# The last residual of a fused diffusion layer: new row factors, and tiles dealt out anew to three engines

## The chip, the cores and the metric

The program runs on one core of a Trainium2 chip. The metric is the device time of one launch, in microseconds (us), as a median over runs. The engines are named as in the profile: PE is TensorE (PEld its weight loads), DVE is VectorE, ACT is ScalarE, POOL is GpSimd, and SP is the engine that here only issues DMA transfers.

## What is computed

One layer of a hybrid backbone over 384 tokens (128 context, 256 latent) of width 2048: modulation, a mixing sub-layer, and a SwiGLU feed-forward sub-layer. Only its last line matters here:

```python
ff = (jax.nn.silu(h @ lw['w_ffn_gate']) * (h @ lw['w_ffn_up'])) @ lw['w_ffn_down']
x = x + ga2 * rmsnorm(ff, lw['norm_post_ffn'])
```

with `rmsnorm(x, g) = x * rsqrt(mean(x * x) + EPS) * g`, the mean over the 2048 channels of a token. So each token needs one factor, 1/sqrt(mean of ff squared), and every channel of that token is multiplied by it before it is added to x.

## The kernel before

Everything is held transposed: channels on the 128 partitions, the 384 tokens along the free dimension. A tensor of 2048 channels is 16 tiles of 128x384 fp32, written `x1(k)` (the residual) and `acc(k)` (the accumulated FFN output), k = 0 to 15. Both live in SBUF in two halves of eight tiles, named Chi and Clo for x1, Bhi and Blo for acc in the profile.

All large products are made of float32r hi and lo parts, three matmuls each, at line 253 (`gemm`); tiles of weights are loaded by SP and split by ScalarE (line 220) and VectorE (line 221). The FFN runs in 11 chunks of 512 hidden channels; `down` (line 1140 on) adds each chunk's share to `acc`. In the last chunk it does more, per tile k: VectorE makes `ff` (line 1152) and adds the square of an earlier tile, kept in the list `late`, to the running sum `qs[0]` (line 1154); ScalarE makes the square of this tile (line 981; for the last tile VectorE makes it, line 1157), then multiplies ff by the modulation's gate and the norm's gain and puts that back into `acc(k)` (line 1163).

Then comes the tail, lines 1182 to 1231. Engines work in the order in which the program lists their instructions; from the last loop on SP too (`manual_schedule`), so a DMA that waits holds up the DMAs behind it on its queue.

- `put(k)` lets TensorE copy x1(k) into a PSUM bank, by a product with the identity, for those six tiles that it will finish itself.
- `tok_sum` sums over the partitions: three products per source tile, each with a block of 128 tokens as the stationary operand and a column of ones moving, so that column t of `pst` holds the sums of token block t. `rsqrt` is a square root on ScalarE (line 298) and a reciprocal on VectorE (line 299); its result `r3` has tokens on partitions.
- `rows` turns r3 round: VectorE makes three diagonal blocks from the identity (line 305), and TensorE multiplies a matrix of ones with them (line 306), which leaves the 384 factors, the same on all partitions, in the PSUM tile `prow`. ScalarE copies them to SBUF as `rr` (line 1199).
- Each tile k is then finished in one of three ways. Six on TensorE: VectorE multiplies acc(k) by the factors (line 1205), TensorE adds that to the preloaded bank through the identity (line 1209), ScalarE copies the bank to x1(k) (line 1210) and issues the store. Four on GpSimd: product and add, both in SBUF. Six on VectorE alone: product and add. Only the first product reads `prow`; all others read `rr`.
- A loop of 18 steps deals out VectorE's 12 products and 6 adds, with GpSimd's tiles between them; SP issues the stores of the ten tiles that aren't TensorE's, in the order of that loop. A store is one tile, 192 KB.

[...]

Of the kernel before, what the change touches and what calls it, by code (L numbers as in the profile page):

```python
# [11 lines left out]
F32 = mybir.dt.float32  # L12
# [6 lines left out]
ENG = mybir.EngineType  # L19

P = 128
D = 2048
KT = D // P
TC = 128
TL = 256
T = TC + TL
# [66 lines left out]
def tile_step(ctx: ExitStack, tc: tile.TileContext, a, o):  # L93
    nc = tc.nc
    PE, ACT, DVE, POOL, SP = nc.tensor, nc.scalar, nc.vector, nc.gpsimd, nc.sync
# [15 lines left out]
    ident = const.tile([P, P], F32, name="ident")  # L111
# [23 lines left out]
    def halves(t):  # L135
        tl = [actp.tile([P, 8, T], F32, tag=f"{t}_{n}", name=f"{t}{n}") for n in ("hi", "lo")]
        return lambda k: tl[k // 8][:, k % 8, :], tl
# [102 lines left out]
    def grab(hold=False):  # L240
        w = take()
        push(hold=hold)
        return w

    def step(side):
        if side is not None:
            next(side, None)

    def gemm(dst, w, x, kts, n=P, n0=0, k0=0, first=True, last=True):

        for k in range(kts):
            for j, (wi, xi) in enumerate(((0, 0), (0, 1), (1, 0))):
                PE.matmul(  # L253
                    dst, w[wi][:, k * n + n0 : k * n + n0 + P], x[xi][:, k0 + k, :],
                    start=first and k == 0 and j == 0, stop=last and k == kts - 1 and j == 2,
                )
# [26 lines left out]
    def tok_sum(dst, *src):  # L283

        for t in range(3):
            for n, s in enumerate(src):
                PE.matmul(
                    dst[:, t : t + 1], s[:, t * P : (t + 1) * P], ones[:, 0:1],
                    start=n == 0, stop=n == len(src) - 1,
                )  # L290
# [6 lines left out]
    def rsqrt(dst, src, scale):  # L297
        ACT.activation(dst, src, AF.Sqrt, bias=eps_t[:, 0:1], scale=scale)
        DVE.reciprocal(dst, dst)

    def rows(pool, dst, r, bufs=2):

        dg = pool.tile([P, T], F32, tag="sq", name="diag", bufs=bufs)
        for t in range(3):
            DVE.tensor_scalar_mul(dg[:, t * P : (t + 1) * P], ident, r[:, t : t + 1])
        PE.matmul(dst, ones, dg, start=True, stop=True)
# [4 lines left out]
    pss = ctx.enter_context(tc.tile_pool(name="pss", bufs=5, space=PSUM))  # L311
    with ExitStack() as s:
# [107 lines left out]
        qs = [pa.tile([P, T], F32, name=f"qsA{n}") for n in range(2)]  # L420
        for k in range(KT):
            sq = qs[k] if k < 2 else scr[:, 4 + k % 4, :]
# [16 lines left out]
        for kb in range(KT):  # L439
# [17 lines left out]
            hf = scr[:, kb % 8, :]  # L457
# [323 lines left out]
    with ExitStack() as s:  # L781
# [155 lines left out]
        mT, late = None, []  # L937
        for b, i in mix_order:
# [9 lines left out]
            else:  # L948
# [5 lines left out]
                g, y = gates.pop((b, i))  # L954
# [13 lines left out]
    x1, x1t = halves("C")  # L968
    with ExitStack() as s:
        pe = s.enter_context(tc.tile_pool(name="pe", bufs=2))  # L970
# [6 lines left out]
        qs = [pe.tile([P, T], F32, tag=f"qs{n}", name="qs", bufs=1) for n in range(3)]  # L977

        def add_sq(total, src, first):
            sq = total if first else pe.tile([P, T], F32, tag="sq", name="sq")  # L980
            ACT.activation(sq, src, AF.Square)
            return None if first else sq
# [40 lines left out]
        pst = [pss.tile([P, 8], F32, tag="side", name=f"pst{n}") for n in range(2)]  # L1023
# [3 lines left out]
        r = pe.tile([P, 2, 3], F32, name="r12", bufs=1)  # L1027
        rsqrt(r[:, 0, :], pst[0][:, 0:3], 1.0 / D)
        rr = pe.tile([P, 2, T], F32, tag="rr", name="rr", bufs=1)
        prow = pss.tile([P, T], F32, tag="side", name="prow")  # L1030
# [66 lines left out]
        for k in range(KT + 1):  # L1097
# [6 lines left out]
            if k:  # L1104
                if k % 8 == 1:
                    hw = [take() for _ in range(HEAD)]
                for n, (j, m) in enumerate(((0, 0), (1, 0), (0, 1))):
                    for u in range(HEAD):
                        PE.matmul(
                            hp[u], hw[u][j][:, ((k - 1) % 8) * P : ((k - 1) % 8 + 1) * P], h2[m][:, k - 1, :],  # L1110
                            start=k == 1 and n == 0, stop=k == KT and n == 2,
# [8 lines left out]
        acc, _ = None, None  # L1120
# [19 lines left out]
        def down(c, i, side):  # L1140
            w = grab()
            for q in range(2):
                p = pss.tile([P, T], F32, tag="side", name="pdn")
                gemm(p, w, hid[c], FC, n=2 * P, n0=q * P)
                k = 2 * i + q
                if c == 0:
                    ACT.copy(acc(k), p)
                elif c < NFC - 1:
                    DVE.tensor_add(acc(k), acc(k), p)  # L1149
                else:  # L1150
                    f = pe.tile([P, T], F32, tag="hf", name="ff", bufs=4)
                    DVE.tensor_add(f, acc(k), p)
                    if late:
                        DVE.tensor_add(qs[0], qs[0], late.pop())
                    if k == KT - 1:
                        sq = pe.tile([P, T], F32, tag="sq", name="sq")
                        DVE.tensor_mul(sq, f, f)
                    else:
                        sq = add_sq(qs[0], f, k == 0)
                    if k:  # L1160
                        late.append(sq)
                    for lo, hi, cd in segs:
                        ACT.mul(acc(k)[:, lo:hi], f[:, lo:hi], mods[:, 5, k, cd : cd + 1])
            step(side)
# [3 lines left out]
        for kind, c, j in ffn_order[HEAD:]:  # L1168
            if kind == "d":
                if c == 0 and j == 0:  # L1170
                    acc, _ = halves("B")
                if c == NFC - 1 and j == 0:
                    for _ in ada:
                        pass
                    ACT.activation(tmp1, eps_t, AF.Sqrt)
                    qs[0] = pe.tile([P, T], F32, tag="qs0", name="qsE", bufs=1)
                down(c, j, ada)
            else:
                proj(psm, h2, lambda p: dst_of[kind](p, c, j), ada)


        py = {}

        def put(k, pool, tag):
            py[k] = pool.tile([P, T], F32, tag=tag, name="py")
            PE.matmul(py[k], ident, x1(k), start=True, stop=False)

        for k in (4, 5, 8):
            put(k, psm, "mm")
        pst = pss.tile([P, 4], F32, tag="side", name="pstE")  # L1190
        tok_sum(pst[:, 0:3], qs[0], late.pop())
        r3 = pe.tile([P, 3], F32, name="r3", bufs=1)
        rsqrt(r3, pst[:, 0:3], 1.0 / D)
        for k in (9, 14):
            put(k, pss, "side")
        prow = pss.tile([P, T], F32, tag="side", name="prowE")
        rows(pe, prow, r3)
        rr = pe.tile([P, T], F32, tag="rr", name="rrE", bufs=1)
        ACT.copy(rr, prow)
        put(15, pss, "side")  # L1200
        ys = {}

        def scale(k, eng, tag, bufs, r):
            ys[k] = pe.tile([P, T], F32, tag=tag, name="yE", bufs=bufs)
            eng.tensor_mul(ys[k], acc(k), r)  # L1205

        def finish(k, eng):
            if k in py:
                PE.matmul(py[k], ident, ys[k], start=False, stop=True)
                ACT.copy(x1(k), py[k])  # L1210
            else:
                eng.tensor_add(x1(k), x1(k), ys[k])
            (ACT if k in py else SP).dma_start(o["yT"][:, k, :], x1(k))

        def step_y(n, k):
            if k in py:
                scale(k, DVE, "sq", 2, rr if n else prow)
                finish(k, DVE)
            elif k in ys:
                finish(k, DVE)  # L1220
            else:
                scale(k, DVE, "hf", 4, rr)

        s.enter_context(tc.manual_schedule(engines={ENG.PE, ENG.Activation, ENG.DVE, ENG.Pool, ENG.SP}))
        pool_ks = [2, 3, 10, 11]
        for n, k in enumerate((4, 0, 5, 0, 8, 1, 9, 1, 14, 6, 15, 6, 7, 12, 7, 12, 13, 13)):
            if n % 4 == 1 and pool_ks:
                scale(pool_ks[0], POOL, "t1", 3, rr)
            step_y(n, k)
            if n % 4 == 1 and pool_ks:  # L1230
                finish(pool_ks.pop(0), POOL)


# [76 lines left out]
```

## Time and profile before

| | us |
|---|---|
| median of the runs | 2067.26 (3 runs, 2064.86 to 2067.55) |
| profiled execution | 2063.03, of which the span of its instructions 2061.3 |
| last product of the FFN ends | 2037.68 |
| first product with the row factors starts | 2043.58 |
| VectorE's last add starts | 2057.70 |

| engine | busy us | share |
|---|---|---|
| PE | 2031.1 | 99% |
| DVE | 1273.7 | 62% |
| ACT | 780.5 | 38% |
| POOL | 45.4 | 2% |

The profile is of one execution. A line of a timeline gives start, duration, engine, source line, operation, and output<-inputs with their shapes; in brackets stands how long the engine was idle before and what ended that. A group's row gives the shortest, median and longest duration in nanoseconds. A row of the windows gives a stretch of time, its length, the busy time of PE, PEld, DVE, ACT and POOL in it with their instructions, the granted clock of TensorE, the mean busy share of the 16 DMA engines and the GB/s that they moved. A matmul of plain fp32 operands is two rows. A row that is marked xN stands for N instructions, from the first one's start to the last one's end, if nothing of that engine lies between.

### The profile page before, as it was taken

The numbers are of one execution on the slowest core, as the hardware profiler recorded it, in microseconds if no ns is written. First come the engines' busy times: TensorE is split into PE (matmuls) and PEld (weight loads), VectorE is DVE, ScalarE is ACT, GpSimd is POOL, SyncE is SP. The second block draws the span as 40 slices with busy tenths as digits, with TensorE's granted clock in tenths as the row PEclk, the third lists the DMA queues.
The fourth block names the chain that finished last, engine by engine and source line by source line (L and its number), as shares of the span: only waits on it lengthen the run. The fifth ranks groups of instructions, "written<-read, shape, count | busy, mean of one in ns | idle before, by whom it ended". The sixth has DMA issues, their size and how long they took to land.

```text
span 2061.3 us, 30173 instructions
## 1 busy us (share of the span) xinstructions
PE 2031.1 (99%) x12250; PEld 1959.8 (95%) x12250; DVE 1273.7 (62%) x1662; ACT 780.5 (38%) x1161; POOL 45.4 (2%) x52
## 2 busy tenths in 40 slices
PE   8999999999999999998999999999999999999997
PEld 5779999999999999988999999999999999999996
DVE  5669787888667787867444545453545454544346
ACT  3233555454346554445333223222222222232234
POOL 0000000000000000023000000000000000000001
PEclk9999999999999999999999999999999999999999
DMA  9977666767546685632444444443444444433332
GB/s 387 352 274 262 196 223 226 243 206 263 203 154 224 237 294 179 193 124 74 162 145 142 154 153 143 143 151 126 143 143 154 144 151 146 149 127 123 123 133 82
DMA packets 112167, 373.64 MB, mean 181 GB/s; under 512 B 13627, under 2 KB 32251, under 8 KB 107932
## 3 DMA queue, kind: packets, MB, share of 16 engines
q1 hardware_dynamic: 111164, 370.54, 52.5%
q8 instruction: 96, 1.57, 0.3%
q10 hardware_dynamic: 864, 1.18, 0.2%
q14 instruction: 43, 0.35, 0.1%
HBM read 358.04 MB, written 13.63 MB: 180 GB/s over the span
## 4 chain that ended last, share of the span: by engine, by line
PE 96%; DVE 2%; issue 0%; DMA 0%; ACT 0%; SPq 0%; DVEq 0%; ACTq 0%
PE pmm L253 66%; PE pdn L253 18%; PE pv L387 3%; PE pf L253 2%; PE pgm L370 2%; PE px L405 1%; DVE yE L1205 0%; PE po L592 0%; DMA Clo<-in_xT 0%; PE pr L538 0%; PE z L614 0%; DVE z L1068 0%; PE dl L592 0%; PE pgm L468 0%; DVE z L1062 0%
## 5 line engine op out<-in xcount | busy, mean ns | idle before, releaser
L253 PE MATMUL pmm<-A_hi,whi 128*128 128x384 f32 x2480 | 833.3, 336 | 0.0
L253 PE MATMUL pmm<-A_hi,wlo 128*128 128x384 f32 x2480 | 829.1, 334 | 0.0
L253 PE MATMUL pmm<-A_lo,whi 128*128 128x384 f32 x2480 | 829.0, 334 | 0.0
L221 DVE TENSOR_TENSOR wlo<-raw,whi 128x1024 fp32r<-128x1024 f32 x433 | 529.1, 1224 | 433.1 <-ACT whi L220 424.1
L220 ACT CAST whi<-raw 128x1024 fp32r<-128x1024 f32 x436 | 457.6, 1050 | 616.9 <-PE pmm L253 212.0
L253 PEld LDWEIGHTS pmm<-A_hi,whi 128*128 128x128 f32 x2480 | 465.6, 188 | 4.8 <-issue 1.6
L253 PEld LDWEIGHTS pmm<-A_lo,whi 128*128 128x128 f32 x2480 | 465.7, 188 | 0.0
L253 PEld LDWEIGHTS pmm<-A_hi,wlo 128*128 128x128 f32 x2480 | 465.6, 188 | 0.0
L530 DVE SCALAR_TENSOR_TENSOR adacc<-adaw,spad,adacc 128x1024 f32<-128x1024 f32 x240 | 297.0, 1279 | 0.9 <-DMA adaw<-in_w_ada 0.7
L253 PE MATMUL pdn<-hid_hi,whi 128*128 128x384 f32 x704 | 235.2, 334 | 0.0
L253 PE MATMUL pdn<-hid_hi,wlo 128*128 128x384 f32 x704 | 235.1, 334 | 0.0
L253 PE MATMUL pdn<-hid_lo,whi 128*128 128x384 f32 x704 | 235.1, 334 | 0.0
L253 PEld LDWEIGHTS pdn<-hid_hi,whi 128*128 128x128 f32 x704 | 132.2, 188 | 0.4 <-issue 0.4
L253 PEld LDWEIGHTS pdn<-hid_lo,whi 128*128 128x128 f32 x704 | 132.2, 188 | 0.0
L253 PEld LDWEIGHTS pdn<-hid_hi,wlo 128*128 128x128 f32 x704 | 132.2, 188 | 0.0
L279 ACT CAST hid_hi<-hfE 128x384 fp32r<-128x384 f32 x44 | 22.6, 513 | 160.4 <-DVE hfE L1132 160.4
L1132 DVE TENSOR_TENSOR hfE<-sg,pmm 128x384 f32<-128x384 f32 x44 | 24.4, 555 | 81.1 <-PE pmm L253 80.5
L1124 ACT ACTIVATE sg<-pmm 128x384 f32<-128x384 f32 x44 | 21.7, 492 | 133.3 <-PE pmm L253 133.3
L1149 DVE TENSOR_TENSOR Blo<-Blo,pdn 128x384 f32<-128x384 f32 x72 | 39.5, 553 | 46.6 <-PE pdn L253 46.6
L1149 DVE TENSOR_TENSOR Bhi<-Bhi,pdn 128x384 f32<-128x384 f32 x72 | 39.2, 550 | 34.1 <-PE pdn L253 33.9
L253 PE MATMUL pmm<-o_hi,whi 128*128 128x384 f32 x128 | 42.8, 335 | 0.0
L253 PE MATMUL pmm<-o_lo,whi 128*128 128x384 f32 x128 | 42.8, 334 | 0.0
(297 smaller groups left out, 1575.6 us busy)
## 6 DMA issues: line engine op xcount, KB each, us to landing
adaw<-in_w_ada SPq DMA_DIRECT2D x128, 512.0 KB
raw<-in_w_g SPq DMA_DIRECT2D x88, 512.0 KB
raw<-in_w_u SPq DMA_DIRECT2D x88, 512.0 KB
raw<-in_w_d SPq DMA_DIRECT2D x88, 512.0 KB
slab<-in_w_ada SPq DMA_DIRECT2D x32, 1024.0 KB
raw<-in_w_gate SPq DMA_DIRECT2D x64, 512.0 KB
raw<-in_w_in SPq DMA_DIRECT2D x44, 512.0 KB
raw<-in_w_out SPq DMA_DIRECT2D x32, 512.0 KB
```

Of the source, the lines that this page charges most:

```text
L220: ACT.copy(hi, raw)
L221: eng.tensor_sub(lo, raw, hi.bitcast(F32))
L253: PE.matmul(dst, w[wi][:, k * n + n0 : k * n + n0 + P], x[xi][:, k0 + k, :], start=first and k == 0 and j == 0, stop=last and k == kts - 1 ...
L279: ACT.copy(hi, src)
L370: PE.matmul(pgv[q : q + 32, :], spad[:, k, :], slab[k // (KT // 2)][:, k % (KT // 2), :], start=k < 4, stop=k >= KT - 4,)
L387: PE.matmul(pv[2 * t + g], hT[x_][:, kb, t * P : (t + 1) * P], w_[:, g * 512 : (g + 1) * 512], start=kb == 0 and j == 0, stop=kb == KT - 1 ...
L405: PE.matmul(px, w_[:, u * P : (u + 1) * P], hT[x_][:, kb, :], start=j == 0, stop=j == 2)
L530: DVE.scalar_tensor_tensor(acc[:, c, :], w, spad[:, k, c : c + 1], acc[:, c, :], op0=ALU.mult, op1=ALU.add,)
L1124: ACT.activation(sgs[j], p, AF.Silu)
L1132: DVE.tensor_mul(hf, sgs.pop(j), p)
L1149: DVE.tensor_add(acc(k), acc(k), p)
```

## The change

Four things change, all of them behind the FFN's last product.

- The square of the last tile is no longer joined by the square before it on VectorE: `qs[0]` stays without the square of tile 14, and TensorE sums `qs[0]` and that square into columns 0 to 2 of `pst`, the last square into columns 4 to 6. VectorE copies the first three columns to r3 and adds the others.
- The tiles are dealt out anew: 0, 4, 8, 1, 5, 9 to TensorE, 2, 6, 10, 14 to GpSimd, 3, 7, 11, 12, 13, 15 to VectorE. Four preloads, where there were three, stand ahead of the token sums, and two behind them.
- The diagonal blocks are gone. The factors are spread by three products of 128 columns, in which the stationary operand is one column of r3, repeated 128 times, and the identity moves.
- VectorE reads the factors from the PSUM tile `prow` in all its products. Where it finishes a tile alone, its product goes to a PSUM tile `pys`, from which the add reads it. GpSimd reads `rr` as before. GpSimd's eight instructions are listed first, then six rounds of one tile of TensorE's and one of VectorE's; SP's stores come in the order V V G V V G V G V G (V a tile of VectorE's, G one of GpSimd's).

```diff
-                    if late:
+                    if late and k < KT - 1:
                         DVE.tensor_add(qs[0], qs[0], late.pop())
...
-        for k in (4, 5, 8):
+        pe_ks, pool_ks, dve_ks = [0, 4, 8, 1, 5, 9], [2, 6, 10, 14], [3, 7, 11, 12, 13, 15]
+        for k in pe_ks[:3]:
             put(k, psm, "mm")
-        pst = pss.tile([P, 4], F32, tag="side", name="pstE")
-        tok_sum(pst[:, 0:3], qs[0], late.pop())
+        put(pe_ks[3], pss, "side")
+        pst = pss.tile([P, 8], F32, tag="side", name="pstE")
+        prow = pss.tile([P, T], F32, tag="side", name="prowE")
+
+        last_sq = late.pop()
+        tok_sum(pst[:, 0:3], qs[0], *late)
+        tok_sum(pst[:, 4:7], last_sq)
         r3 = pe.tile([P, 3], F32, name="r3", bufs=1)
-        rsqrt(r3, pst[:, 0:3], 1.0 / D)
-        for k in (9, 14):
+        DVE.tensor_copy(r3, pst[:, 0:3])
+        DVE.tensor_add(r3, r3, pst[:, 4:7])
+        rsqrt(r3, r3, 1.0 / D)
+        for k in pe_ks[4:]:
             put(k, pss, "side")
-        prow = pss.tile([P, T], F32, tag="side", name="prowE")
-        rows(pe, prow, r3)
+        for t in range(3):
+            PE.matmul(
+                prow[:, t * P : (t + 1) * P], r3[:, t : t + 1].to_broadcast([P, P]), ident, start=True, stop=True,
+            )
         rr = pe.tile([P, T], F32, tag="rr", name="rrE", bufs=1)
         ACT.copy(rr, prow)
-        put(15, pss, "side")
...
+        pys = pss.tile([P, T], F32, tag="side", name="pys")
+        def on_pool(k):
+            y = pe.tile([P, T], F32, tag="t1", name="yP", bufs=3)
+            POOL.tensor_mul(y, acc(k), rr)
+            POOL.tensor_add(x1(k), x1(k), y)
+
+        def on_pe(k):
+            y = pe.tile([P, T], F32, tag="hf", name="yE", bufs=4)
+            DVE.tensor_mul(y, acc(k), prow)
+            PE.matmul(py[k], ident, y, start=False, stop=True)
+            ACT.copy(x1(k), py[k])
+            store(k, ACT)
+
+        def on_dve(k):
+            DVE.tensor_mul(pys, acc(k), prow)
+            DVE.tensor_add(x1(k), x1(k), pys)
+            store(k, SP)
+
+        for k in pool_ks:
+            on_pool(k)
+        for n in range(6):
+            on_pe(pe_ks[n])
+            on_dve(dve_ks[n])
+            if n in (1, 3, 4, 5):
+                store(pool_ks.pop(0), SP)
```

More of the change, by code (lines that the diff above doesn't have):

```diff
@@ L1198, in tile_step @@
         rr = pe.tile([P, T], F32, tag="rr", name="rrE", bufs=1)
         ACT.copy(rr, prow)
-        put(15, pss, "side")
[L1201 to L1222, printed above, removed]
-        s.enter_context(tc.manual_schedule(engines={ENG.PE, ENG.Activation, ENG.DVE, ENG.Pool, ENG.SP}))
[L1225 to L1231, printed above, removed]
+        pys = pss.tile([P, T], F32, tag="side", name="pys")
@@ new lines, in tile_step, with store @@
+        s.enter_context(tc.manual_schedule(engines={ENG.PE, ENG.Activation, ENG.DVE, ENG.Pool, ENG.SP}))
+        def store(k, eng):
+            eng.dma_start(o["yT"][:, k, :], x1(k))
+        def on_pool(k):
[8 more added lines that the diff above has]
+            store(k, ACT)
```

## The prediction

> **What bounds the kernel now.** First the head of the page and its chain of work: TensorE carries 96% of a 2061.3 us span, and that part is untouched. I then read the chain for the last 30 us, in order of time.
>
> ```profile
> span 2061.3 us, 30173 instructions
> PE 96%; DVE 2%; issue 0%; DMA 0%; ACT 0%; SPq 0%; DVEq 0%; ACTq 0%
> ```
> ```profile
> 2029.87 7.80 PE pdn L253 x45
> ...
> 2043.07 0.49 ACT rrE L1199
> ...
> 2043.58 2.72 DVE yE L1205 x3
> ```
>
> The last FFN product ends at 2037.68; 23.6 us of tail follow, and all edits lie there. It has two halves: the path to the row factors, up to 2043.58, and the scaling with its stores. The timeline of TensorE shows the first half in queue order:
>
> ```profile
> 2037.52 1.45 PE L1186 MATMUL py<-Chi,ident 128*128 128x384 f32 x4
> 2038.80 0.81 PE L1186 MATMUL py<-Clo,ident 128*128 128x384 f32 x2
> 2039.45 0.28 PE L287 MATMUL pstE<-ones,qsE 128*128 128x1 f32 x2
> 2039.59 0.36 PE L287 MATMUL pstE<-ones,sq 128*128 128x1 f32 x2
> 2040.48 0.36 PE L287 MATMUL pstE<-ones,sq 128*128 128x1 f32 x2
> 2040.70 1.54 PE L1186 MATMUL py<-Clo,ident 128*128 128x384 f32 x4
> 2042.12 0.91 PE L306 MATMUL prowE<-diag,ones 128*128 128x384 f32 x2
> ```
>
> Each fp32 product is two rows. The three preloads of x1 take 2037.52 to 2039.45, 0.64 each; the six token sums then follow at (2040.48 - 2039.59)/4 = 0.22 each. VectorE and ScalarE beside them:
>
> ```profile
> 2038.19 0.55 DVE L1154 TENSOR_TENSOR qsE<-qsE,sq 128x384 f32<-128x384 f32 x1
> 2038.65 0.55 DVE L1157 TENSOR_TENSOR sq<-ff 128x384 f32<-128x384 f32 x1
> 2040.88 0.26 ACT L298 ACTIVATE r<-pstE,eps_t 128x3 f32<-128x3 f32 x1 [1.78 <-PE pstE L287]
> 2041.18 0.18 DVE L299 RECIPROCAL r<-r 128x3 f32<-128x3 f32 x1 [1.97 <-ACT r L298]
> 2041.39 0.68 DVE L305 TENSOR_SCALAR diag<-ident,r 128x128 f32<-128x128 f32 x3
> ```
>
> The last square is done at 2039.20, before TensorE has finished its preloads (2039.45). So the sums wait for TensorE's own queue, not for VectorE.
>
> The second half: VectorE's own timeline, GpSimd's work by tile, and the DMA's share by windows.
>
> ```profile
> 2043.58 0.55 DVE L1205 TENSOR_TENSOR yE<-Bhi,prowE 128x384 f32<-128x384 f32 x1 [1.52 <-ACT rrE L1199]
> 2046.23 1.34 DVE L1212 TENSOR_TENSOR Chi<-Chi,yE 128x384 f32<-128x384 f32 x1
> 2047.49 1.35 DVE L1205 TENSOR_TENSOR yE<-Blo,rrE 128x384 f32<-128x384 f32 x1
> 2054.31 0.55 DVE L1205 TENSOR_TENSOR yE<-Blo,rrE 128x384 f32<-128x384 f32 x1
> 2054.78 0.54 DVE L1212 TENSOR_TENSOR Chi<-Chi,yE 128x384 f32<-128x384 f32 x1
> 2057.13 0.54 DVE L1205 TENSOR_TENSOR yE<-Blo,rrE 128x384 f32<-128x384 f32 x1
> 2057.70 0.56 DVE L1212 TENSOR_TENSOR Clo<-Clo,yE 128x384 f32<-128x384 f32 x1
> ```
> ```profile
> 2043.62 1.00 POOL L1205 TENSOR_TENSOR yE<-Bhi,rrE 128x384 f32<-128x384 f32 x1 [1083.43 <-ACT rrE L1199]
> 2052.32 1.19 POOL L1212 TENSOR_TENSOR Clo<-Clo,yE 128x384 f32<-128x384 f32 x1
> ```
> ```profile
> 2055.20:2056.00 0.80, 0.80 (x2) 0.34 (x1) 0.80 (x3) 0.34 (x1) 0.00 (x0) 0.50 0.00 0
> 2056.20:2060.00 3.80, 0.70 (x2) 0.00 (x0) 2.03 (x5) 0.48 (x1) 0.00 (x0) 0.50 1.00 360
> 2060.00:2061.30 1.30, 0.00 (x0) 0.00 (x0) 0.00 (x0) 0.00 (x0) 0.00 (x0) 0.50 0.01 1
> ```
>
> While GpSimd works (2043.62 to 2053.51), a VectorE step with two SBUF inputs takes 1.35 at a spacing of 1.27; afterwards 0.55 at 0.47, or 0.57 where a step reads its predecessor's result (2057.13 to 2057.70). The one step with a PSUM input under GpSimd, at 2043.58, took 0.55. And the end is not VectorE's alone: the DMA engines run full (share 1.00, 360 GB/s) for the last 3.80 us, seven stores issued from 2055.35 on:
>
> ```profile
> 2055.35 0.33 SPq L1213 DMA_DIRECT2D out_yT<-Chi  x1
> 2058.29 0.33 SPq L1213 DMA_DIRECT2D out_yT<-Clo  x1
> ```
>
> So a 192 KB store costs 3.80/7 = 0.54, its data move some 0.88 after the issue, and 1.35 of waits and barrier follow the last byte. Check: 2055.35 + 0.88 + 7 x 0.537 + 1.35 = 2061.34.
>
> **The change, part by part: the path to the row factors.**
>
> Last square apart: one 0.47 spacing leaves VectorE, but the sums waited for TensorE, so it is worth nothing. What it adds is on the path. A fourth preload stands ahead of the sums: +0.64. Three more sums: 3 x 0.22 = +0.67. Both groups of sums go into one PSUM tile, and the built order signals them once, after the ninth; so the copy of the first group can't run early. The sums end at 2040.84 + 1.31 = 2042.15. Copy and add of 128x3 are new links; the nearest row is the reciprocal (start 2041.18, next step 2041.39), so 0.20 each, 0.40. Square root and reciprocal stay at 2041.36 - 2040.84 = 0.52: r3 is ready at 2043.07.
>
> Broadcast columns: the three diagonal steps (0.68) go. But the queue has two preloads between the sums and the row products. The ninth sum starts at 2040.48 + 1.31 = 2041.79, the preloads at 2042.01, and TensorE is free at 2043.30. The row products wait for that, not for r3: start +1.18 against 2042.12. They are three products of 128 columns, six rows; the nearest is
>
> ```profile
> 1929.10 0.38 PE L547 MATMUL ptm<-ident,adev 128*128 128x128 f32 x2
> L547 PE MATMUL ptm<-ident,adev x16: 270/271/328, 234.5 to 1929.2; 128*128 128x128 f32 x16
> ```
>
> 0.38 - 0.27 = 0.11 from row to row: 5 x 0.11 + 0.27 = 0.82 for the 0.91 of before, done at 2044.12. No row shows a stationary operand that repeats one column. Bounds: as any other, 0.11 a row, or 0.34, the longest a weight load took here (one at the lowered clock, below), +1.4. I take 0.11, since it is of this shape at full clock.
>
> ```profile
> L1209 PEld LDWEIGHTS py<-yE,ident x12: 186/189/338, 2044.2 to 2055.4; 128*128 128x128 f32 x12
> ```
>
> VectorE's first step still waits for ScalarE's copy, which reads the same PSUM tile: 2043.58 - 2043.03 = 0.55 as before. The scaling begins at S = 2044.67, **1.09 later**.
>
> **The scaling.** VectorE has 18 steps, as before: in each of six rounds a product for TensorE, a product into PSUM, and an add that reads it. None has two SBUF inputs. Spacings 0.47, 0.60 (start to end 0.55 and the signal; 0.57 is the row) and 0.47: a round is 1.54. GpSimd keeps four tiles; undisturbed it needs about 1.01 a step:
>
> ```profile
> L1052 POOL TENSOR_TENSOR Clo<-t,Clo x3: 993/1009/1013, 932.7 to 947.3; 128x384 f32<-128x384 f32 x3
> ```
>
> so 2.1 a tile, S + 8.4 at the end, below VectorE's S + 9.3. SP's queue takes the stores in a written order, two of VectorE's or one, then one of GpSimd's; the last is GpSimd's, behind VectorE's last at S + 9.36, so it issues at S + 9.79 (0.43 between issues). ScalarE's chain from a product to its store is 2.07 (2043.58 to the issue at 2045.65):
>
> ```profile
> 2045.65 0.38 ACTq L1213 DMA_DIRECT2D out_yT<-Chi  x1
> ```
>
> By the last issue alone the gain would be (2058.29 - 2044.67 - 9.79) = 3.83. But the same 16 stores now come in 8.1 us instead of 12.6, and at 0.537 they need 8.6. VectorE's fourth store is ready at S + 3 x 1.54 + 1.66 = S + 6.28 and finds the engines idle; nine stores follow back to back: 6.28 + 0.88 + 9 x 0.537 = S + 11.99, and 1.35 to the end. Span: 2044.67 + 13.34 = 2058.0, **3.3 us shorter**, of which the faster scaling gives 4.4 and the longer row path takes 1.1. SP keeps ten stores and ScalarE six, so the new order of tiles is free by itself: GpSimd's first store, ready at S + 2.1, waits on SP for VectorE's second until S + 3.6, and those after S + 6.3 wait behind the full DMA anyway.
>
> What a PSUM output costs VectorE no row shows. Bounds: as PSUM inputs, nothing (0.547 in the first row below, 0.545 with SBUF inputs), or 0.3 more per round. Then the gain is 3.4 (dependent step at 0.57) or 2.2 (a round of 1.75). I take the row.
>
> ```profile
> L1149 DVE TENSOR_TENSOR Bhi<-Bhi,pdn x72: 545/547/555, 1174.7 to 1987.8; 128x384 f32<-128x384 f32 x72
> L1052 DVE TENSOR_TENSOR Clo<-t,Clo x5: 543/545/551, 943.0 to 955.0; 128x384 f32<-128x384 f32 x5
> ```
>
> [...]
>
> **The sum.** The profiled execution took 2063.03 (span 2061.3), which becomes 2059.7. It lies 4.2 below the median of the runs shown, 2067.26; I carry the difference over: 2067.26 - 3.3 = 2064.0.
>
> **Rivals.** (a) The row path comes no later than before, because preloads and sums overlap more than their spacings say. For it: weight loads do run ahead. Against it: TensorE showed no gap from 2037.52 to 2040.84. S falls to 2043.58, gain 4.4: 2062.9; with the diagonal's 0.7 gained as well, 2062.2.
> (b) The slowdown beside GpSimd stays for steps that write or read PSUM. Place: the first 9.9 us of the scaling, eight steps at 1.27; then ten at the free pace; VectorE ends at S + 15.4, the last store at S + 15.9, span 2063.3: 2.0 longer, 2069.3. It turns into a loss once VectorE's mean spacing passes 0.68 (forecast 0.51). For it: the 1.35 rows. Against: the row at 2043.58. [...]
> (c) The broadcast stationary is slow (+1.4): gain 1.9, 2065.4.
>
> **How the numbers follow.** About 0.2% (4.1 us) is what a measurement of this kernel tells from no change. Forecast 0.60, own range 2063 to 2065.3; (a) 0.24; (b) 0.07; (c) 0.06; anything else 0.03. The runs of before spread over 2.7, so each end takes another 1.3: low 2061.0 from (a), high 2067.0 from (c) and the dearer PSUM; (b) is left out. Faster by over 0.2% needs 4.1 saved: (a) and the fast edge of the forecast with the runs' spread, 0.38. Within: 0.55. Slower: 0.07, the upper part of (b) and the unknown.
>
> **What would show it.** The first scaling step at about 2044.7, not before 2043.6; row products starting when the two preloads end; VectorE's 18 steps at 0.55 without a 1.3 among them; GpSimd near 1.0 a step; a DMA share of 1.0 in the last 4.8 us. Steps of 1.3 beside GpSimd, or an idle DMA at the end, would make it wrong.

## The result, and the profile after

| | before | after |
|---|---|---|
| median of the runs, us | 2063.78 (19 runs, 2061.45 to 2067.55) | 2061.11 (19 runs, 2059.12 to 2063.21) |
| ratio to before | | 0.9983, 95% interval 0.9977 to 0.999 |
| profiled execution, us (span) | 2063.03 (2061.3) | 2059.12 (2057.3) |

By the ratio the kernel became faster by 0.17%; the two medians by themselves differ by 2.67 us, 0.13%. The 19 runs of before include the three on which the prediction's anchor rested; the median of all of them lies 3.5 us under the median of those three.

Runs of one kernel spread over 4 to 6 us, and most of that spread arises ahead of the edits: in the profiles of this case the FFN's last matmul row starts anywhere between 2036.67 and 2044.13. All readings below therefore count from the start of that row, called zero. In these two rows of TensorE's timeline (start, duration), zero is 2037.34 before, and after:

```profile
2037.34 0.34 PE L253 MATMUL pdn<-hid_hi,wlo 128*128 128x384 f32 x1
```
```profile
2036.67 0.34 PE L253 MATMUL pdn<-hid_hi,wlo 128*128 128x384 f32 x1
```

The tail is what follows zero up to the end of the span: 2061.3 - 2037.34 = 23.96 before, 2057.3 - 2036.67 = **20.63** after. It is 3.33 shorter. (A span is given to a tenth of a us, so rounding alone moves a tail by up to 0.05; S has no such error.) The first scaling step, S, starts 6.24 after zero before and 7.43 after it now. So the row path is 1.19 later, and the scaling half went from 17.72 to 13.20.

TensorE's timeline of after, in the order of its queue, shows the longer row path:

```profile
2036.84 1.45 PE L1186 MATMUL py<-Chi,ident 128*128 128x384 f32 x4
2038.13 0.81 PE L1186 MATMUL py<-Clo,ident 128*128 128x384 f32 x2
2038.78 0.81 PE L1186 MATMUL py<-Chi,ident 128*128 128x384 f32 x2
2039.42 0.28 PE L287 MATMUL pstE<-ones,qsE 128*128 128x1 f32 x2
...
2040.45 1.03 PE L287 MATMUL pstE<-ones,sq 128*128 128x1 f32 x8
2041.35 0.89 PE L1186 MATMUL py<-Chi,ident 128*128 128x384 f32 x2
2042.08 0.81 PE L1186 MATMUL py<-Clo,ident 128*128 128x384 f32 x2
2042.72 0.83 PE L1205 MATMUL prowE<-ident,r 128*128 128x128 f32 x6
```

With two rows to a product these are four preloads up to 2039.42, nine sums up to 2041.35 (four of them not shown), two preloads, and then the row products with no gap in front of them. VectorE's timeline has the new copy and add, and then the scaling:

```profile
2041.53 0.16 DVE L1199 COPY r<-pstE 128x3 f32<-128x3 f32 x1 [3.34 <-PE pstE L287]
2041.72 0.16 DVE L1200 TENSOR_TENSOR r<-r,pstE 128x3 f32<-128x3 f32 x1
2042.24 0.18 DVE L299 RECIPROCAL r<-r 128x3 f32<-128x3 f32 x1 [0.36 <-ACT r L298]
2044.10 0.55 DVE L1224 TENSOR_TENSOR yE<-Bhi,prowE 128x384 f32<-128x384 f32 x1 [1.68 <-ACT rrE L1209]
2044.57 0.56 DVE L1230 TENSOR_TENSOR pys<-Bhi,prowE 128x384 f32<-128x384 f32 x1
2045.16 0.55 DVE L1231 TENSOR_TENSOR Chi<-Chi,pys 128x384 f32<-128x384 f32 x1
2045.63 0.55 DVE L1224 TENSOR_TENSOR yE<-Bhi,prowE 128x384 f32<-128x384 f32 x1
...
2052.79 0.55 DVE L1231 TENSOR_TENSOR Clo<-Clo,pys 128x384 f32<-128x384 f32 x1
```

The factors are ready at 2042.42 (2042.24 + 0.18), 0.30 ahead of the row products: these wait for TensorE's queue. In the scaling no step takes 1.3 any more; a round is 2045.63 - 2044.10 = 1.53. GpSimd beside it, by groups (mean ns behind the comma), and the DMA by windows (the last three columns are granted clock, DMA share, GB/s):

```profile
L1219 POOL TENSOR_TENSOR yP<-Bhi,rrE 128x384 f32<-128x384 f32 x2 | 2.0, 1000 | 1084.6 <-ACT rrE L1209 1084.6
L1220 POOL TENSOR_TENSOR Clo<-Clo,yP 128x384 f32<-128x384 f32 x2 | 2.0, 997 | 0.2
```
```profile
2051.20:2056.00 4.80, 1.44 (x4) 0.30 (x2) 2.07 (x5) 0.96 (x2) 1.04 (x2) 0.94 1.01 365
2056.20:2057.30 1.10, 0.00 (x0) 0.00 (x0) 0.00 (x0) 0.00 (x0) 0.00 (x0) 0.50 0.00 0
```

GpSimd runs at 1.00 a step, the pace that it has undisturbed (1.01 in the prediction's row), and the DMA is full for the last 4.8 us in which anything moves.

### The profile page after: what moved, and what is told of

Read it like the earlier page. It is cut to its first block, busy times and chain, and to the rows that moved or that the text cites. A ratio compares the mean times of both kernels' runs of the same rounds, so it can differ in the third digit from the quotient of the medians.

```text
span 2057.3 us, 30190 instructions
## 1 busy us (share of the span) xinstructions
PE 2029.1 (99%) x12260; PEld 1959.9 (95%) x12260; DVE 1266.6 (62%) x1660; ACT 780.2 (38%) x1161; POOL 43.6 (2%) x52
## 4 chain that ended last, share of the span: by engine, by line
PE 96%; DVE 2%; DMA 1%; issue 0%; ACT 0%; SPq 0%; DVEq 0%; ACTq 0%
PE pmm L253 66%; PE pdn L253 18%; PE pv L387 3%; PE pf L253 2%; PE pgm L370 1%; PE px L405 1%; PE pmm L1109 0%; PE po L592 0%; DMA Clo<-in_xT 0%; PE pr L538 0%; DMA slab<-in_w_ada 0%; PE z L614 0%; DVE z L1068 0%; PE dl L592 0%; PE px L822 0%
```

## The experiments

All numbers of a run count from its own zero. The profiles were taken on several chips; the changed kernel, profiled on two occasions, shows the same S both times.

| kernel | S | tail |
|---|---|---|
| before | 6.24 | 23.96 |
| after | 7.43 | 20.63 |
| after, product in SBUF | 7.44 | 22.87 |
| before, broadcast columns alone | 6.12 | 23.88 |
| after, last square joined | 6.76 | 19.95 |
| after, fourth preload behind the sums | 7.43 | 20.79 |
| after, half stores | 7.44 | 20.08 |
| after, diagonal blocks again | 7.98 | 21.22 |
| short path | 5.39 | 18.58 |
| short path, square joined | 6.91 | 20.55 |
| short path, one preload ahead | 5.16 | 18.41 |
| short path, again | 4.78 | 18.45 |
| one preload ahead, again | 5.15 | 18.37 |
| after, again | 7.43 | 20.86 |

**The product in SBUF instead of PSUM.** VectorE's six solitary products go to an SBUF tile, so that the adds have two SBUF inputs.

```diff
-        pys = pss.tile([P, T], F32, tag="side", name="pys")
...
         def on_dve(k):
+            pys = pe.tile([P, T], F32, tag="sq", name="ysb", bufs=2)
             DVE.tensor_mul(pys, acc(k), prow)
```

> The change, but VectorE's own product goes to SBUF instead of PSUM, so the add has two SBUF inputs again. Times are counted from the start of the last FFN matmul row to the end of the span; the kernel before needs 23.96 us, the changed kernel 20.63, with the first scaling step at 6.24 and 7.43. Theory (a VectorE step with two SBUF inputs is held up while GpSimd works, one with a PSUM input is not): the adds take 1.0 to 1.35 us while GpSimd works, GpSimd's steps 1.2 instead of 1.0, a round 2.2 instead of 1.53, and the tail about 23.0. Rival (the shorter rounds come from the new order of tiles, or the full DMA engines cover them): the tail stays within 0.3 of 20.63.

Measured: a tail of 22.87, 2.24 worse than after. Of this kernel, from VectorE's and GpSimd's timelines:

```profile
2049.76 0.55 DVE L1230 TENSOR_TENSOR ysb<-Bhi,prowE 128x384 f32<-128x384 f32 x1
2050.34 1.27 DVE L1231 TENSOR_TENSOR Chi<-Chi,ysb 128x384 f32<-128x384 f32 x1
2052.57 1.26 DVE L1231 TENSOR_TENSOR Clo<-Clo,ysb 128x384 f32<-128x384 f32 x1
2054.79 1.26 DVE L1231 TENSOR_TENSOR Clo<-Clo,ysb 128x384 f32<-128x384 f32 x1
2057.02 0.56 DVE L1231 TENSOR_TENSOR Clo<-Clo,ysb 128x384 f32<-128x384 f32 x1
```
```profile
2048.89 1.35 POOL L1219 TENSOR_TENSOR Chi<-Chi,yP 128x384 f32<-128x384 f32 x1
2050.20 0.99 POOL L1218 TENSOR_TENSOR yP<-Bhi,rrE 128x384 f32<-128x384 f32 x1
```

Three of the six adds take 1.26 to 1.27 instead of 0.55, and 3 x 0.71 = 2.13 is nearly the whole loss. The first add also ran beside GpSimd, but took 0.56: it started at 2048.82, just ahead of GpSimd's add at 2048.89, and there GpSimd's add was the one held up, to 1.35. GpSimd's other adds take 1.19. The last two of VectorE's ran when GpSimd was done. TensorE's granted clock also fell to 0.5 in this run, so that its product of the fourth round took 1.65 instead of 0.91; no step of VectorE's scaling waits for TensorE in its timeline; what share of the 2.24 the clock has, if any, isn't shown. The product's own price is 0.55 into SBUF and 0.55 to 0.56 into PSUM: the output in PSUM costs nothing that the trace can show, and it is what takes the adds out of GpSimd's way. In these rows three of the four adds with two SBUF inputs that ran beside GpSimd are held up, to 1.26 and 1.27, and the products, which have one, take 0.54 to 0.56 throughout.

**The broadcast columns alone, in the kernel before.**

```diff
         prow = pss.tile([P, T], F32, tag="side", name="prowE")
-        rows(pe, prow, r3)
+        for t in range(3):
+            PE.matmul(
+                prow[:, t * P : (t + 1) * P], r3[:, t : t + 1].to_broadcast([P, P]), ident, start=True, stop=True,
+            )
```

> The kernel before with one edit: the factors are spread by the broadcast columns instead of the diagonal blocks. Theory (the row products then wait for the two preloads that stand ahead of them on TensorE): they start 0.14 us sooner and take 0.82 instead of 0.91, the first scaling step comes at 6.0 after the last FFN row instead of 6.24, and the tail is 23.7 instead of 23.96. Rival (the diagonal steps were wholly on the path): first scaling step at 5.4, tail 23.2. Rival (a repeated column is slow to load as weights): the row products take over 1.2, and nothing is gained.

Measured: S 6.12, tail 23.88, 0.12 and 0.08 under before, half or less of what was expected. TensorE's timeline of this kernel, whose zero is 2041.12:

```profile
2044.49 1.54 PE L1186 MATMUL py<-Clo,ident 128*128 128x384 f32 x4
2045.86 0.83 PE L1198 MATMUL prowE<-ident,r 128*128 128x128 f32 x6
```

The row products start 4.74 after zero, where before's started 4.78 after it: 0.04 sooner, not 0.14. The three diagonal steps of 0.68 had been hidden behind the two preloads. What is left is the products themselves, 0.83 for 0.91. Six rows in 0.83, where the prediction's row of this shape gave 0.82, also say that a stationary operand that repeats one column costs no more than another here.

**The diagonal blocks put back, in the changed kernel.**

```diff
+        rows_dg = pe.tile([P, T], F32, tag="sq", name="diag", bufs=2)
         for t in range(3):
-            PE.matmul(
-                prow[:, t * P : (t + 1) * P], r3[:, t : t + 1].to_broadcast([P, P]), ident, start=True, stop=True,
-            )
+            DVE.tensor_scalar_mul(rows_dg[:, t * P : (t + 1) * P], ident, r3[:, t : t + 1])
+        PE.matmul(prow, ones, rows_dg, start=True, stop=True)
```

> The changed kernel with the diagonal blocks instead of the broadcast columns. Theory: the three diagonal steps (0.71) end 0.45 after TensorE has done its preloads, and the one product takes 0.91 instead of 0.83; the first scaling step comes at 7.95 instead of 7.43, tail 21.15. Rival (preloads cover the diagonal): 7.5 and 20.7.

Measured: S 7.98, tail 21.22, as the theory expected: here the broadcast columns are worth 0.55 in S and 0.59 in the tail. TensorE now waits for the diagonal, which it doesn't in the kernel before:

```profile
2043.69 0.91 PE L1207 MATMUL prowE<-diag,ones 128*128 128x384 f32 x2 [0.30 <-DVE diag L1206]
```

The same edit is worth 0.1 in one kernel and 0.6 in the other: in the second the factors come 1.7 later against zero (the reciprocal starts 5.57 after it, before 3.84) while the preloads end only 1.3 later.

**The last square joined again.** VectorE adds the square of tile 14 as it did, TensorE makes six sums, and copy and add fall away.

```diff
-                    if late and k < KT - 1:
+                    if late:
                         DVE.tensor_add(qs[0], qs[0], late.pop())
...
-        tok_sum(pst[:, 0:3], qs[0], *late)
-        tok_sum(pst[:, 4:7], last_sq)
+        tok_sum(pst[:, 0:3], qs[0], last_sq)
         r3 = pe.tile([P, 3], F32, name="r3", bufs=1)
-        DVE.tensor_copy(r3, pst[:, 0:3])
-        DVE.tensor_add(r3, r3, pst[:, 4:7])
-        rsqrt(r3, r3, 1.0 / D)
+        rsqrt(r3, pst[:, 0:3], 1.0 / D)
```

> The changed kernel, but the last square is joined as before: VectorE adds the square of tile 14, six token sums instead of nine, no copy and no add behind them. Theory (summing the last square apart costs three sums on TensorE and two small steps, and gains nothing): the row products start 0.67 sooner, when TensorE is free, the first scaling step comes at 6.76 instead of 7.43, the tail is 19.96 instead of 20.63. Rival (the square apart takes a VectorE step off the path): the first scaling step comes 0.47 later, tail 21.1.

Measured: S 6.76 and tail 19.95, 0.67 and 0.68 under after. This is the three sums, 3 x 0.22. Copy and add are worth nothing here, since the row products wait for the preloads. In the order of the changed kernel, the part that sums the last square apart is a loss of 0.68, so this kernel's tail is shorter than those of both given ones.

**The fourth preload moved behind the sums.**

```diff
-        put(pe_ks[3], pss, "side")
...
-        for k in pe_ks[4:]:
+        for k in pe_ks[3:]:
             put(k, pss, "side")
```

> The changed kernel with one preload moved: the fourth stands behind the token sums, not ahead of them. Theory (the row products wait for all that stands ahead of them on TensorE, six preloads and nine sums, in whatever order): the factors' column is ready 0.64 sooner, but the first scaling step stays at 7.43 (within 0.1) and the tail at 20.63. Rival (what counts is when the sums end): first scaling step at 6.8, tail 20.0.

Measured: S 7.43, unchanged as expected: ahead of the sums or behind them, the preload stands in TensorE's queue ahead of the row products. The tail is 20.79, 0.16 longer. TensorE's timeline of this kernel shows three products that run together to 4.18, where in the profile of after each takes 0.91 with gaps between; the same rows come back, without any edit, in a second profile of the changed kernel (second fence):

```profile
2047.27 4.18 PE L1224 MATMUL py<-yE,ident 128*128 128x384 f32 x6 [0.61 <-DVE yE L1223]
```
```profile
2048.41 4.17 PE L1225 MATMUL py<-yE,ident 128*128 128x384 f32 x6 [0.61 <-DVE yE L1224]
```

In both the granted clock stood at 0.5 for most of that time. The second profile has S 7.43 and a tail of 20.86, 0.23 above the first one. So the 0.16 is no more than what comes without the edit, and tails of single profiles are good to 0.2 and no better. The second profile was taken with this expectation, in which "the two above" are the short path and the one with one preload ahead, both described below:

> The changed kernel once more, beside the two above on one chip. Tail 20.6 and the scaling 7.4 after the start of the FFN's last row if the readings of single profiles hold; a tail more than 0.2 away from 20.6 would say that single profiles can't be compared to a tenth. By time, the short paths should stand about 2 us (0.1%) under it.

Measured: S as expected, the tail 0.26 above 20.6. The times stand with the short paths below.

**Half stores.** Only the first half of each stored tile's tokens goes out; the other half of the output is left out.

```diff
-            eng.dma_start(o["yT"][:, k, :], x1(k))
+            eng.dma_start(o["yT"][:, k, 0 : T // 2], x1(k)[:, 0 : T // 2])
```

> The changed kernel, but every store of the last stage writes only the first 192 of the 384 tokens, half the bytes; the other half of the output is left out. Times from the start of the last FFN matmul row. Theory (the end is set by nine stores back to back on full DMA engines): with half the bytes each fits between its neighbours, the end is the last issue plus the way of one small store, and the tail is 19.5 us instead of 20.63. Rival (the end is the last issue plus a fixed way): only the last store's own transfer gets shorter, 0.27, tail 20.35.

Measured: tail 20.08, 0.55 under after, between the two values expected. The last stores of SP and ScalarE issue together, and the DMA is no longer full:

```profile
2052.00:2054.00 2.00, 1.39 (x4) 0.30 (x2) 1.95 (x4) 0.48 (x1) 1.00 (x1) 1.00 0.62 196
2054.00:2056.00 2.00, 0.00 (x1) 0.00 (x0) 0.10 (x1) 0.48 (x1) 0.00 (x0) 1.00 0.72 224
2056.00:2057.50 1.50, 0.00 (x0) 0.00 (x0) 0.00 (x0) 0.00 (x0) 0.00 (x0) 0.63 0.05 16
```

The expected 19.5 took 0.27 for a half store and forgot that two of them are issued at once at the end. By the windows such a store costs more than half: 96 KB at some 310 GB/s (196/0.62 and 224/0.72 are 316 and 311) are 0.32, and two of these end 0.4 later than one of 0.27. So in the changed kernel the end is set by the queue on the DMA, but half the bytes are worth only 0.55: without the queue the end is set by the last steps of VectorE and ScalarE, which issue the last stores.

**A short path.** No preload stands ahead of the sums, one between sums and row products, the others behind; the last square is still summed apart, but into a PSUM tile of its own, so that the copy of the first sums needn't wait for the last ones.

```diff
-        for k in pe_ks[:3]:
-            put(k, psm, "mm")
-        put(pe_ks[3], pss, "side")
-        pst = pss.tile([P, 8], F32, tag="side", name="pstE")
+        pst = pss.tile([P, 4], F32, tag="side", name="pstE")
+        pst2 = pss.tile([P, 4], F32, tag="side", name="pstE2")
...
-        tok_sum(pst[:, 4:7], last_sq)
         r3 = pe.tile([P, 3], F32, name="r3", bufs=1)
         DVE.tensor_copy(r3, pst[:, 0:3])
-        DVE.tensor_add(r3, r3, pst[:, 4:7])
+        tok_sum(pst2[:, 0:3], last_sq)
+        DVE.tensor_add(r3, r3, pst2[:, 0:3])
         rsqrt(r3, r3, 1.0 / D)
-        for k in pe_ks[4:]:
-            put(k, pss, "side")
+        put(pe_ks[0], psm, "mm")
...
         ACT.copy(rr, prow)
+        for k in pe_ks[1:3]:
+            put(k, psm, "mm")
...
             on_pe(pe_ks[n])
+            if n < 3:
+                put(pe_ks[n + 3], pss, "side")
```

> The changed kernel with TensorE's queue in another order: no preload ahead of the token sums, one between the sums and the row products, the other five behind the row products; the last square is summed into a bank of its own, so that the copy of the first sums is done before. Theory (the path to the factors is TensorE's queue): the first scaling step at 4.5 after the last FFN row instead of 7.43, the same scaling behind it, tail 17.7 instead of 20.63; 2.9 us (0.14%) faster than the changed kernel, ratio to the kernel before 0.997. Rival (the preloads, now between the products, hold up VectorE's rounds or the stores): the first step as early, but rounds over 1.6 and a tail over 18.5.

Measured: median 2057.68 us, ratio to before 0.9965 (0.9953 to 0.9977); S 5.39 and tail 18.58 in the profile. Both are 0.9 later than expected. The rounds stay at 1.53 and the scaling behind S keeps its length (18.58 - 5.39 = 13.19, in the changed kernel 13.20), so the rival, preloads that hold up the rounds, is out. TensorE's timeline of this kernel (zero 2037.52):

```profile
2040.71 1.65 PE L1202 MATMUL prowE<-ident,r 128*128 128x128 f32 x6
2042.15 1.49 PE L1186 MATMUL py<-Chi,ident 128*128 128x384 f32 x2
```

The row products take 1.65 instead of 0.83 and the preload behind them 1.49 instead of 0.81, at a granted clock of 0.5. The 0.82 that the row products lost is nearly the whole miss. The kernel was run once more:

> The kernel of the short path once more (no preload ahead of the token sums), to see whether its clock fall belongs to the kernel or to the moment. Theory, the fall belongs to the thin work: granted clock near 0.5 somewhere between 2039 and 2045 again, row products about 1.6, tail from the start of the FFN's last row again 18.4 to 18.8. Rival, it was the moment: clock 1.0 through the row path, row products 0.83, scaling starting 4.5 after that row, tail 17.7.

Measured: S 4.78, tail 18.45. The clock fell again, but 1.0 later against zero, at the end of the row products, so neither value expected for them came:

```profile
2043.94 1.04 PE L1202 MATMUL prowE<-ident,r 128*128 128x128 f32 x6
```

Here the fall met the two preloads behind them, 1.49 each; ScalarE's first store was issued 3.52 after S, where the changed kernel has 2.07, and the scaling took 13.67. So S is 0.61 better than in the first profile, and the tail only 0.13.

**One preload ahead of the sums in the short path**, to see whether it keeps the clock up:

```diff
+        put(pe_ks[0], psm, "mm")
         pst = pss.tile([P, 4], F32, tag="side", name="pstE")
...
-        put(pe_ks[0], psm, "mm")
+        put(pe_ks[1], psm, "mm")
...
-        for k in pe_ks[1:3]:
+        for k in pe_ks[2:3]:
             put(k, psm, "mm")
```

> The kernel with TensorE's short queue, but one preload goes ahead of the token sums again, one stands between the sums and the row products, four behind. In the kernel with no preload ahead TensorE's granted clock fell to 0.5 some 2.7 us after the last FFN product, before the row products, which took 1.65 instead of 0.83. Theory (the clock falls because nine token sums, products of one column, are all that TensorE has done since; a preload of 384 columns ahead of them keeps it up): the clock stays at 1.0 until the row products are through, they take 0.83, the first scaling step comes at 5.1 after the last FFN row (5.39 with no preload ahead), tail 18.3 (18.58). Rival (the clock falls a fixed time after the last FFN product, whatever preloads there are): row products of 1.65 again, first step at 6.0, tail 19.2.

> The kernel with one preload ahead of the sums once more. Theory (one preload is enough to keep the clock): clock 1.0 through the row path, scaling 5.2 after the start of the FFN's last row, tail 18.4. Rival (the fall comes at any time with little work on TensorE): clock near 0.5 within the row path, scaling 6.0 or later, tail 19.2 or more.

Measured: S 5.16 and tail 18.41, and in the second profile 5.15 and 18.37, with the clock at 1.0 through both row paths. These are the values expected; that the preload is what kept the clock up is not shown by them (see the last section). VectorE's and TensorE's timelines of the first profile:

```profile
2042.23 0.18 DVE L299 RECIPROCAL r<-r 128x3 f32<-128x3 f32 x1 [0.36 <-ACT r L298]
2042.46 0.94 PE L1203 MATMUL prowE<-ident,r 128*128 128x128 f32 x6
```

The row products now start 0.05 behind the reciprocal's end (2042.41): in the short path the factors come last, and no longer TensorE's queue.

Median 2058.93 us, ratio to before 0.9971 (0.9962 to 0.9981). In the last comparison, on one chip, where the kernel before took 2064.92, the three kernels stood as follows: short path 2059.23 us, 0.9975 (0.9963 to 0.9986); one preload ahead 2059.53, 0.9973 (0.9963 to 0.9983); changed kernel 2060.12, 0.9976 (0.9968 to 0.9985). By their tails the short paths are 2.0 to 2.5 better than the changed kernel; by time they stand 0.6 to 0.9 under it, and the intervals overlap almost wholly. The "about 2 us" of the expectation is thus not confirmed by time. Whether something ahead of zero takes part of it back, or the spread hides it, stays open.

**The short path with the square joined.**

```diff
-                    if late and k < KT - 1:
+                    if late:
                         DVE.tensor_add(qs[0], qs[0], late.pop())
...
-        tok_sum(pst[:, 0:3], qs[0], *late)
+        tok_sum(pst[:, 0:3], qs[0], last_sq)
...
-        tok_sum(pst2[:, 0:3], last_sq)
-        DVE.tensor_add(r3, r3, pst2[:, 0:3])
-        rsqrt(r3, r3, 1.0 / D)
+        rsqrt(r3, pst[:, 0:3], 1.0 / D)
```

> The kernel with TensorE's short queue (no preload ahead of the sums), and the last square joined as in the kernel before: one more VectorE add, six sums instead of nine, no copy and no add behind them. Theory (with nothing ahead of them the sums wait for VectorE, so that here the square apart does take 0.47 off the path, and three sums of the last square are all that is left behind it): first scaling step at 5.3 against 4.5 with the square apart, tail 18.5 against 17.7. Rival (three sums, copy and add cost as much as they save, as they do behind the preloads): first step at 4.5 or sooner.

Measured: S 6.91 and tail 20.55, where 5.3 and 18.5 were expected. TensorE's timeline of this kernel:

```profile
2040.70 0.38 PE L287 MATMUL pstE<-ones,qsE 128*128 128x1 f32 x2 [1.11 <-DVE qsE L1154]
2044.12 1.49 PE L1198 MATMUL prowE<-ident,r 128*128 128x128 f32 x6
```

Without preloads ahead of them the sums wait 1.11 for VectorE's joining add, and then the clock fell. Against the two profiles of the short path the square apart is worth 1.5 and 2.1 in S; the fall of the clock, at another place in each, holds a part of that which these runs don't separate. So behind four preloads the square apart costs 0.67 in S, and with none it gains.

## Why the prediction was right or wrong

Two steps of the prediction failed, the anchor of the time and the bound on what can be measured; its mechanism held.

**Wrong: the anchor.** The step "I carry the difference over: 2067.26 - 3.3 = 2064.0" took the profiled execution to lie 4.2 under the kernel's median. Over 19 runs it lies 2063.78 - 2063.03 = 0.75 under it. The term was 3.5 us too large, and it isn't the kernel's: a median of three runs was given full trust, of a kernel whose 19 runs spread over 6.1 us. The same sum on the median of the 19 gives 2060.5, and 2061.11 was measured; the medians differ by 2.67 where the sum has 3.3. That 2061.11 lies within the prediction's whole range (2061.0 to 2067.0) all the same is luck: it is outside the range of the forecast itself (2063 to 2065.3), and the low end comes from rival (a), which is out.

**Wrong: what a measurement can tell.** "About 0.2% (4.1 us) is what a measurement of this kernel tells from no change" stood there with no row behind it, and put a gain of 3.3 us (0.16%) on the side of no change. The measured ratio is 0.9983, hence the size was right, but its interval reaches from 0.9977 to 0.999: 19 runs on each side resolve about 0.07%. The forecast of no measurable change fails on this bound and not on a mechanism.

**Right: the sign and size of the tail**, 3.3 forecast and 3.33 in the profiles; a second profile of the changed kernel gives 23.96 - 20.86 = 3.1.

**Row path.** Forecast 1.09 later, measured 1.19. The row products did wait for TensorE's two preloads and not for the factors. They took 0.83 (forecast 0.82), and in the kernel before the diagonal turned out to be hidden behind the preloads. The missing 0.1: the two preloads behind the sums took 2042.72 - 2041.35 = 1.37, not 2 x 0.64. The prediction's own row of four such matmul rows (1.54) already had this. Rival (a), a row path that isn't later, is out. "One 0.47 spacing leaves VectorE ... worth nothing" was right, and so were the three sums, 0.67 by the kernel with the square joined. The 0.64 of the fourth preload counts, but not its place: moved behind the sums it left S where it was, since the row products wait for six preloads either way, where before they waited for five. The 0.40 for copy and add was priced rightly (2041.53 to 2041.91 with the signal) and is hidden: with them only the sums' 0.67 came back. Up to the row products the path of the changed kernel is TensorE's queue from end to end.

**Scaling.** Forecast 4.4 shorter, measured 17.72 - 13.20 = 4.52. Rounds of 1.53 (1.54 forecast), GpSimd at 1.00 (1.01), the last add ending 9.24 after S (9.3), the DMA full for 4.8 us. Last bytes at about 2056.1, or S + 12.0, against S + 11.99. VectorE itself gained more: its last add ended 14.68 after S before (2057.70 + 0.56 - 2043.58), 5.44 later than now; the DMA, full for 4.8 us at the end where it was for 3.8, takes the rest back. The product in SBUF shows that about 2.2 of the 4.52 are due to the PSUM tile `pys`. The rest, 2.3, falls to the products that read `prow` and to the new deal together; no run separates these two. Rival (b), a slowdown that stays for steps with PSUM, is out: all 18 steps take 0.55 to 0.56.

**The price of PSUM for VectorE.** The prediction took nothing, with 0.3 a round as the dear bound (its round of 1.75, from which it took the gain of 2.2, is only 0.21 more; the two don't fit together, and neither came up). No run shows the 0.3, the 1.75 or that gain of 2.2: the rows give 0.55 to 0.56 with a PSUM input and a PSUM output alike, and rounds of 1.53.

**The broadcast stationary.** Six rows in 0.83: rival (c) is out.

## What to carry to other kernels

Steps with two SBUF inputs on VectorE beside GpSimd were freed here by sending the intermediate through PSUM: three of six adds took 0.55 instead of 1.26 to 1.27, which was worth some 2.2 us, at no cost that the trace shows. The worth of a step on a path that ends in an engine's queue depends on what stands ahead of it in that queue: the broadcast columns gained 0.1 or 0.6, the square apart lost 0.7 or gained, by what else stood on the path, the preloads above all. A forecast's absolute time should be anchored on as many runs as there are, and where an edit sits in a short tail, that tail should be compared from a mark of its own.

## What the runs showed that was not expected

TensorE's granted clock fell to 0.5 in the tail, at a place that differs from run to run, and where the fall ended again ahead of the last stores it had one length, about 3.4 us, or twice that. Windows of 0.8 us at its two edges (the third number from the end is the clock), of the short path, its repetition, the repeated changed kernel, and the short path with the square joined:

```profile
2040.00:2040.80 0.80, 0.80 (x3) 0.15 (x2) 0.29 (x2) 0.30 (x1) 0.00 (x0) 0.77 0.00 0
2043.20:2044.00 0.80, 0.80 (x3) 0.38 (x2) 0.77 (x3) 0.00 (x0) 0.75 (x1) 0.60 0.00 0
```
```profile
2044.00:2044.80 0.80, 0.80 (x7) 0.80 (x8) 0.00 (x0) 0.00 (x0) 0.00 (x0) 0.89 0.00 0
2048.00:2048.80 0.80, 0.80 (x4) 0.54 (x3) 0.77 (x3) 0.26 (x1) 0.72 (x2) 0.97 0.68 246
```
```profile
2048.00:2048.80 0.80, 0.39 (x1) 0.39 (x2) 0.80 (x2) 0.31 (x1) 0.80 (x2) 0.82 0.04 13
2051.20:2052.00 0.80, 0.80 (x2) 0.50 (x2) 0.77 (x3) 0.38 (x1) 0.72 (x2) 0.55 1.01 359
```
```profile
2041.60:2042.40 0.80, 0.80 (x7) 0.80 (x6) 0.00 (x0) 0.00 (x0) 0.00 (x0) 0.68 0.00 0
2048.00:2048.80 0.80, 0.80 (x3) 0.50 (x2) 0.77 (x3) 0.00 (x0) 0.80 (x2) 0.56 0.18 65
```

A mean of 0.77 in the first window, between the 1.0 and 0.5 of the windows beside it, means that the clock fell after 0.54 x 0.8, at 2040.43; by 0.60 in the second it rose at 2043.84. That is 3.41 us. In the same way the next two give 2044.62 to 2048.05 (3.43) and 2048.51 to 2051.92 (3.41), and the last one 2041.89 to 2048.70, which is 6.81, about 2 x 3.41. What sets these lengths and places no run shows. In the three profiles that have no preload ahead of the sums the fall came within or right behind the row path (1.0 apart in two profiles of one kernel), and it was not seen there in any of the others; whether the thin sums cause it these few runs don't settle. Its price went by what it met: about 0.6 in S where it met the row products (5.39 against 4.78); where it met only products of the scaling, the tail was some 0.2 longer (20.79 and 20.86 against 20.63).
